# A decode step whose score blocks are turned by VectorE, and whose norm statistics use one small product

## The chip, the cores and the metric

The kernel runs on one core of a Trainium2 chip. The metric is the device time of one execution in microseconds (us). A change of under 0.2% (about 6 us here) can't be told from no change by the measurement that is used.

## The reference

One decoder layer is computed twice: for a prompt of 2048 tokens, and for 8 sequences of 4 new tokens each that look back on 8192 cached tokens. Cut to what matters here:

```python
def rms_norm(x, g):            # mean over the channels of one token
    y = x * lax.rsqrt(jnp.mean(x * x, axis=-1, keepdims=True) + EPS)
    return y * g

def diff_attend(q, k, v, q_pos, k_pos, lam):      # 4 heads, two components c
    s = jnp.einsum('bqhcd,bkhcd->bhcqk', q, k) * (HEAD_DIM ** -0.5)
    s = s - alibi_slopes()[None, :, None, None, None] * dist
    pr = jax.nn.softmax(jnp.where(k_pos <= q_pos, s, -jnp.inf), axis=-1)
    w = pr[:, :, 0] - lam * pr[:, :, 1]
    return jnp.einsum('bhqk,bkhe->bqhe', w, v)

def mixer(xn, lp, ...):
    z = xn @ lp['w_in']                            # q, k, v, and the two halves of a gated unit u
    o = diff_attend(...)                           # past keys and values come from pages
    y_attn = rms_norm(o, lp['g_subln']) * (1.0 - lam_init)          # per head
    c = causal_depthwise_conv(u_ext, lp['w_dw'], lp['b_dw'])        # 31 taps
    y_conv = silu(layer_norm(c, lp['ln_conv_g'], lp['ln_conv_b']))
    return concatenate([y_attn, y_conv]) @ lp['w_out'], ...

def decoder_layer(x, pe, lp, ...):
    h = x + rms_norm(mixer(rms_norm(x, lp['g_pre_mix']), ...), lp['g_post_mix'])
    f = square(relu(rms_norm(h, lp['g_pre_ffn']) @ lp['w_ff1'])) @ lp['w_ff2']
    h = h + rms_norm(f, lp['g_post_ffn'])
    return h + sigmoid(h @ lp['w_ple_gate']) * (pe @ lp['w_ple'])
```

## The kernel before

All activations lie with the channel on the partitions and the token along the free axis, so a norm needs a sum over partitions. Products in full precision are made as three products of two halves each (`mm3`: lines L233, L234, L235), the halves coming from ScalarE (a rounded copy, L120) and VectorE (the rest, L121).

The order of the work is written out by hand. There are three stages. The first (to about 520 us) is the input projection, with `zp` as its PSUM tiles, of which there are four; the convolution, the norm of the four 512-token blocks (`square`, `stat`, `spread`) and the decode tokens' projection run beside it as generators that are advanced a step at a time. The second (to about 1048 us) is the prompt's attention: 64 rows of score tiles (L1214 on TensorE, L1219 on VectorE), turned by TensorE (`tp`, L1278) and multiplied with the values (`ov`, L233 to L235). Its work is a list of pieces; after each piece `advance` gives credit to the decode generator and moves the oldest `subln` by one step. The third is the dense part in five groups of 416 tokens (`mm` tiles): output projection, two MLP products, embedding and gate, with the norms `norm_a` and `norm_f` and the convolution's norm `convln` as side generators.

The decode attention is a generator (`decode`) that runs in the second and third stage. For each of the 8 sequences it visits 16 units of 4 pages: first the keys (`ds`, L992), then after the softmax the values (`dacc`, L1064). Scores of 32 rows (head, component, query) are made in four column tiles of TensorE, one per page of a unit. `weights(u)` turns two units' 128x128 score blocks on TensorE (`dwt`, L1046), and ScalarE copies them out (L1048). In the third stage a key visit takes two units at once (`wide_k`), a value visit one. Each visit returns a cost that is taken from the credit.

`Rstd` makes the inverse root of a mean over partitions. `mean` makes four products with a 128x128 block of the squares as the stationary operand and a column of ones as the moving one (L148, `pm`), which leaves one token per partition; `seed` computes the inverse root with an integer guess and three Newton steps on VectorE or GpSimd (L164 to L181); `spread` turns the four columns, broadcast to 128, back with four transposes on TensorE (L188, `rsb`). It is used 40 times at full width: four blocks in stage one, five times in `convln`, 16 times in `subln` (the norm per head and 512 tokens in stage two), and 15 times in `norm_a` and `norm_f`; and twice for the 32 decode tokens.

`subln` is a generator whose steps are counted by `SL = (8, 2, 10, 0, 1, 1, 0)`: square (L1094), 8 steps, mean, 2 steps, seed, 10 steps, spread and scaling (L1110), two steps, rounding and rest, one step, and then two stores of the tile `o` from GpSimd's queue (L1125). `o` has two buffers; ScalarE fills one in two halves from the single `ov` PSUM tile (L1300).

Of the kernel before, what the change touches and what calls it, by code (L numbers as in the profile page):

```python
# [8 lines left out]
F32 = mybir.dt.float32  # L9
# [40 lines left out]
KC = 1000.0, 2000.0  # L50
C1, C2, C3 = 600.0, 200.0, 1000.0
# [3 lines left out]
C_ID, C_G, C_SEL, C_MC, C_C0, C_C1, C_TX = 0, 128, 256, 288, 304, 305, 306  # L55
NCST = 310
# [77 lines left out]
class Rstd:  # L134
# [5 lines left out]
    def __init__(self, nc, pool, bank, ident, n):  # L140
        self.nc, self.pool, self.bank, self.ident = nc, pool, bank, ident
        self.n, self.w = n, min(128, n)
        self.offs = [min(o, n - self.w) for o in range(0, n, self.w)]

    def mean(self, acc, ones):
        self.pm = self.bank("pm")
        for b, o in enumerate(self.offs):
            self.nc.tensor.matmul(self.pm[:self.w, b:b + 1], acc[:, o:o + self.w], ones, start=True, stop=True)  # L148

    def square(self, eng, inv):  # L150
        self.t = self.pool.tile([128, 4], F32, tag="rst", name="rst", bufs=2)[:self.w, :len(self.offs)]
        eng.tensor_tensor(out=self.t, in0=inv, in1=inv, op=ALU.mult)

    def seed(self, eng, inv=None):

        V, w, nb = self.nc.vector, self.w, len(self.offs)

        def small(tag, bufs=2):
            return self.pool.tile([128, 4], F32, tag=tag, name=tag, bufs=bufs)[:w, :nb]

        x, y = small("rsx"), small("rsy", 4)
        t = self.t if inv is not None else small("rst")
        if inv is None:
            V.tensor_scalar(out=x, in0=self.pm[:w, :nb], scalar1=EPS, scalar2=None, op0=ALU.add)  # L164
        else:
            V.scalar_tensor_tensor(out=x, in0=self.pm[:w, :nb], scalar=2.0 ** 22, in1=t, op0=ALU.mult, op1=ALU.mult)
            V.tensor_scalar(out=x, in0=x, scalar1=EPS, scalar2=None, op0=ALU.add)
# [12 lines left out]
        if inv is not None:  # L180
            eng.tensor_tensor(out=y, in0=y, in1=inv, op=ALU.mult)  # L181
# [11 lines left out]
def kernel(  # L193
# [19 lines left out]
    ones_d = cp.tile([128, 1], F32, name="ones_d")  # L213
    ones_c = cp.tile([128, 128], F32, name="ones_c")
    ones_e = cp.tile([128, 1], F32, name="ones_e")
# [8 lines left out]
    ident = cc[:, C_ID:C_ID + 128]  # L224

# [22 lines left out]
    def convln(pool, bank, n0, n, tags, gated=False):  # L248
# [55 lines left out]
        r = Rstd(nc, pool, bank, ident, n)  # L304
        r.mean(acc, ones_c[:, 0:1])
        r.seed(V)
        yield
        yield
        rsb = r.spread()
        rs = cfull[:, 4, :n]  # L310
        S.activation(out=rs, in_=rsb, func=AF.Copy)
        yield
# [69 lines left out]
    with tc.manual_schedule():  # L382
        nc.sync.dma_start(out=vc, in_=vec)
        V.memset(ones_d, 1.0 / 1024)
        V.memset(ones_c, 1.0 / 512)
        S.activation(out=ones_e, in_=ones_d, func=AF.Copy, scale=8.0)
# [5 lines left out]
        with (  # L392
# [68 lines left out]
            def stat(bl):  # L461
                r = rsd_[bl] = Rstd(nc, p1, st_bank, ident, 512)
                r.mean(sums.pop(bl), ones_d)
                r.seed(V)

            def spread(bl):
                t = rs[bl] = p1.tile([128, 512], F32, tag="rs", name="rs", bufs=2)
                S.activation(out=t, in_=rsd_[bl].spread(), func=AF.Copy)
# [16 lines left out]
            def opening():  # L485
# [10 lines left out]
                spread(0)  # L496
                second(4, 6)
                yield
                second(6, 8)
# [4 lines left out]
                yield  # L504
                spread(1)

            def sumsq(bl):
# [5 lines left out]
                stat(bl)  # L513

# [53 lines left out]
            rd = Rstd(nc, p1, dt_bank, ident, NDEC)  # L568
# [9 lines left out]
            def dec_first():  # L578
                V.tensor_copy(rsb_d, rd.spread())
# [1306 lines left out]
```

## Time and profile before

| | us |
|---|---|
| median of 3 runs | 3206.87 (3205.02 to 3211.97) |
| the profiled execution | 3210.34 |
| its span, first to last instruction | 3208.6 |
| TensorE busy | 3084.4 (96%) |
| VectorE busy | 2027.4 (63%) |
| ScalarE busy | 1258.7 (39%) |
| GpSimd busy | 980.5 (31%) |

The profiled execution is 1.7 us longer than its span and 3.5 us above the median. Matmuls are pipelined: one row's duration is its latency, and the distance between two starts is what it takes from the stream.

### The profile page before, as it was taken

The page shows a single profiled execution, that of the slowest core. Times are in us where ns is not written, and L with a number is a line of the kernel's source. Part 1 is how long each engine was busy: PE and PEld are TensorE (multiplying, and loading weights), DVE is VectorE, ACT ScalarE, POOL GpSimd, SP SyncE. Part 2 cuts the span into 40 slices and gives each one's busy share as a digit, 9 for nine tenths or more (in the row PEclk, how much of TensorE's full clock was granted, in tenths as well). Part 3 has the DMA queues.
Part 4 walks back from the last instruction along what each step waited for, and adds up shares of the span by engine and source line. Part 5 has one row for each costly group of instructions (what it writes and reads, how often), then busy time and mean ns, then how long its engine had stood idle before and what let it go on. Part 6 is the DMA issues. An engine that isn't in the chain of part 4 may idle for free.

```text
span 3208.6 us, 55368 instructions
## 1 busy us (share of the span) xinstructions
PE 3084.4 (96%) x19120; PEld 2694.1 (84%) x19120; DVE 2027.4 (63%) x3537; ACT 1258.7 (39%) x2312; POOL 980.5 (31%) x1063
## 2 busy tenths in 40 slices
PE   8999898999999899989999989999989999999998
PEld 6877686867778688879888879889879999999998
DVE  7889664887784667546767536777538444564444
ACT  5333224776675322235322234322334333432233
POOL 2542213776664301123201124210125121320023
PEclk9999898999899999999999999999999999999999
DMA  5444367998887876776876777777654344333334
GB/s 178 135 125 109 110 183 220 293 282 263 251 273 256 291 237 222 250 258 226 288 238 223 237 258 267 243 235 257 210 185 151 123 140 157 125 117 113 118 117 133
DMA packets 316521, 649.45 MB, mean 202 GB/s; under 512 B 45872, under 2 KB 98864, under 8 KB 315984
## 3 DMA queue, kind: packets, MB, share of 16 engines
q1 hardware_dynamic: 313680, 637.53, 61.9%
q0 software_dynamic: 2560, 8.39, 0.7%
q8 instruction: 150, 2.46, 0.3%
q14 instruction: 131, 1.07, 0.1%
HBM read 581.60 MB, written 64.18 MB: 201 GB/s over the span
## 4 chain that ended last, share of the span: by engine, by line
PE 81%; DVE 8%; DMA 4%; issue 3%; ACT 2%; POOL 2%; SPq 1%; POOLq 0%; DVEq 0%; ACTq 0%
PE mm L233 18%; PE mm L235 18%; PE mm L234 18%; PE zp L233 4%; PE zp L234 4%; PE zp L235 4%; PE dacc L1064 3%; PE ds L992 3%; PE scp L1214 3%; PE tp L1278 1%; DVE wlo L121 1%; PE ov L233 1%; PE pm L148 1%; PE ov L235 1%; PE ov L234 1%
## 5 line engine op out<-in xcount | busy, mean ns | idle before, releaser
L121 DVE TENSOR_TENSOR wlo<-wide 128x1024 fp32r<-128x1024 f32 x410 | 528.6, 1290 | 693.7 <-ACT wide L120 304.5
L233 PE MATMUL mm<-bh,wide 128*128 128x416 f32 x1616 | 584.9, 362 | 22.7 <-ACT wide L120 22.7
L234 PE MATMUL mm<-bh,wlo 128*128 128x416 f32 x1616 | 573.9, 355 | 8.7 <-DVE wlo L121 8.5
L235 PE MATMUL mm<-bl,wide 128*128 128x416 f32 x1616 | 573.9, 355 | 0.0
L120 ACT ACTIVATE wide<-wide 128x1024 fp32r<-128x1024 f32 x410 | 430.6, 1052 | 343.5 <-DMA wide<-ff 220.5
L357 POOL TENSOR_TENSOR r<-r 128x416 f32<-128x416 f32 x160 | 156.1, 977 | 1076.2 <-ACT bh L1572 1076.2
L233 PE MATMUL mm<-xh,wide 128*128 128x416 f32 x1280 | 457.2, 357 | 0.0
L235 PE MATMUL mm<-xl,wide 128*128 128x416 f32 x1280 | 450.6, 352 | 2.5 <-DVE xl L1525 2.5
L234 PE MATMUL mm<-xh,wlo 128*128 128x416 f32 x1280 | 447.9, 350 | 1.0 <-DVE wlo L121 1.0
L233 PEld LDWEIGHTS mm<-bh,wide 128*128 128x128 f32 x1616 | 307.4, 190 | 70.8 <-ACT wide L120 28.3
L234 PEld LDWEIGHTS mm<-bh,wlo 128*128 128x128 f32 x1616 | 307.9, 191 | 18.5 <-DVE wlo L121 13.8
L235 PEld LDWEIGHTS mm<-bl,wide 128*128 128x128 f32 x1616 | 307.1, 190 | 4.6
L233 PEld LDWEIGHTS mm<-xh,wide 128*128 128x128 f32 x1280 | 240.1, 188 | 45.7 <-issue 19.3
L245 DVE SCALAR_TENSOR_TENSOR ct<-ct,vc 128x416 f32<-128x416 f32 x360 | 271.1, 753 | 8.4
L233 PE MATMUL zp<-xh,wh 128*128 128x512 f32 x640 | 260.8, 407 | 8.9 <-ACT wh L120 7.7
L234 PE MATMUL zp<-xh,wl 128*128 128x512 f32 x640 | 254.9, 398 | 8.1 <-DVE wl L121 8.1
L1572 ACT ACTIVATE bh<-r 128x416 fp32r<-128x416 f32 x160 | 88.2, 552 | 434.7 <-DVE r L1571 434.7
L235 PE MATMUL zp<-xl,wh 128*128 128x512 f32 x640 | 255.1, 399 | 3.7 <-DVE xl L529 3.7
L235 PEld LDWEIGHTS mm<-xl,wide 128*128 128x128 f32 x1280 | 240.0, 188 | 6.1 <-DVE xl L1525 3.7
L234 PEld LDWEIGHTS mm<-xh,wlo 128*128 128x128 f32 x1280 | 240.7, 188 | 4.6 <-DVE wlo L121 1.6
L1236 ACT ACTIVATE S<-S,m 128x512 f32<-128x512 f32 (+3 forms) x320 | 206.9, 649 | 43.1 <-DVE m L1219 42.3
L245 DVE SCALAR_TENSOR_TENSOR cv<-u,vc,cv 128x416 f32<-128x416 f32 (+1 forms) x240 | 202.9, 845 | 6.9
(251 smaller groups left out, 5184.7 us busy)
## 6 DMA issues: line engine op xcount, KB each, us to landing
wide<-ff SPq DMA_DIRECT2D x320, 512.0 KB, 4.3
kv<-ck SPq DMA_DIRECT2D x512, 256.0 KB, 3.9
kv<-cv SPq DMA_DIRECT2D x512, 256.0 KB, 3.8
wr<-w_in SPq DMA_DIRECT2D x40, 512.0 KB, 5.7
wide<-w_out SPq DMA_DIRECT2D x40, 512.0 KB, 4.7
wide<-gate SPq DMA_DIRECT2D x40, 512.0 KB, 3.3
wide<-qs SPq DMA_DIRECT2D x64, 256.0 KB, 6.4
ya<-ct SPq DMA_DIRECT2D x40, 208.0 KB, 1.9
```

The costliest lines, as they stand in the source:

```text
L120: self.nc.scalar.activation(out=hi, in_=r, func=AF.Copy)
L121: self.lo_eng(self.ns).tensor_tensor(out=lo, in0=r, in1=hi.bitcast(F32), op=ALU.subtract)
L233: T.matmul(out, wh, xh, start=start, stop=False)
L234: T.matmul(out, wl, xh, start=False, stop=False)
L235: T.matmul(out, wh, xl, start=False, stop=stop)
L245: V.scalar_tensor_tensor(out=c, in0=x, scalar=w, in1=c, op0=ALU.mult, op1=ALU.add)
L357: P.tensor_tensor(out=out, in0=a, in1=b, op=ALU.mult)
L992: T.matmul(ps[32 * s:32 * s + 32, o:o + 128 * n], qz[:, b % 2, h, :], ring[:, g:g + 4 * n - 3:4, h * 128:h * 128 + 128], start=(h == 0), s ...
L1064: T.matmul(acc[32 * s:32 * s + 32, :], wts[u // 2 * 2][:, u % 2, 32 * s:32 * s + 32], t[:, s, :], start=(u == 0), stop=(s > 0 and u == UNI ...
L1214: T.matmul(ps[:, :wp], q[:, c, l, r % 2 * 128:r % 2 * 128 + 128], kt[:, n0 % 1024:n0 % 1024 + wp], start=(l == 0), stop=(l == 1),)
L1236: S.activation(out=st_[c][:, o:e], in_=st_[c][:, o:e], func=AF.Exp, scale=-1.0, bias=st_["m"][:, c, last:last + 1], accum_out=st_["lp"][:, ...
L1572: S.activation(out=ah, in_=r, func=AF.Square)
```

## The change

Decode: the four column tiles of a key product no longer take one page each; tile k takes columns 32k to 32k+31 of all four pages. The score block that results can be turned in blocks of 32x32, so `weights` is one VectorE instruction over two units (128x256) in place of two TensorE transposes and a ScalarE copy. A host table (`tabD`) is permuted to match. Value visits take two units when `wide_k` is set, at a cost of 2000 instead of 2 x 1100.

Norms: `Rstd.gather` turns the squares in 32x32 blocks on VectorE and adds up 32 at a time; `mean` is one product of the constant 0/1 matrix `same` with the 16 (13, 4, 1) partial sums; `spread` is one VectorE turn of a broadcast source. The copies of `rsb` out of PSUM by ScalarE go. The callers put steps between `gather` and `mean`: `subln` gets five more steps, `sumsq` three, the opening one; `rstd` and `convln` keep their number. In `subln` the reciprocal of the row sum, which enters the norm, is now laid out by a VectorE product (`inverse`) and goes through the same TensorE product; its square is a VectorE product too, where GpSimd made it before.

```diff
+VC = 1100.0, 2000.0
-    def mean(self, acc, ones):
+    def gather(self, acc, turned, w=16):
+        V, nb = self.nc.vector, self.nb
+        self.part = self.pool.tile([128, w], F32, tag="rsp", name="rsp", bufs=1)
+        V.transpose(turned, acc)
+        V.tensor_reduce(
+            out=self.part[:, :nb], in_=turned.rearrange("p (b f) -> p b f", f=32), axis=AX.X, op=ALU.add
+        )
+        self.w = nb
+    def inverse(self, eng, inv, own):
+        part = self.part[:, self.nb:2 * self.nb].rearrange("p (r g) -> p r g", g=4)
+        eng.tensor_tensor(
+            out=part, in0=inv.rearrange("p (r o) -> p r o", o=1).to_broadcast([128, 4, 4]),
...
+    def mean(self):
         self.pm = self.bank("pm")
-        for b, o in enumerate(self.offs):
-            self.nc.tensor.matmul(self.pm[:self.w, b:b + 1], acc[:, o:o + self.w], ones, start=True, stop=True)
-    def square(self, eng, inv):
...
+        self.nc.tensor.matmul(self.pm[:, :self.w], self.same, self.part[:, :self.w], start=True, stop=True)
...
+            i = small("rsi", 1)
+            V.tensor_copy(i, self.pm[:, nb:2 * nb])
+            V.tensor_tensor(out=t, in0=i, in1=i, op=ALU.mult)
...
-    def spread(self):
-        r = self.bank("rsb")
-        w = self.w
-        for b, o in enumerate(self.offs):
-            self.nc.tensor.transpose(r[:, o:o + w], self.y[:, b:b + 1].to_broadcast([w, 128]), self.ident[:w, :w])
-        return r[:, :self.n]
+    def spread(self, out):
+        nb = self.nb
+        self.nc.vector.transpose(
+            out.rearrange("p (b f) -> p b f", f=32),
+            self.y.rearrange("p (b o) -> p b o", o=1).to_broadcast([128, nb, 32]),
+        )
+        return out
 # opening(): one step later
                 stat(0)
                 second(2, 4)
                 yield
-                spread(0)
                 second(4, 6)
                 yield
+                root(0)
+                spread(0)
                 second(6, 8)
 # decode(), keys
                     for h in range(NH):
-                        for s in range(4):
-                            g = u % RING * 4 + s
+                        for k in range(4):
                             T.matmul(
-                                ps[32 * s:32 * s + 32, o:o + 128 * n], qz[:, b % 2, h, :],
-                                ring[:, g:g + 4 * n - 3:4, h * 128:h * 128 + 128], start=(h == 0), stop=(h == NH - 1),
+                                ps[32 * k:32 * k + 32, o:o + 128 * n], qz[:, b % 2, h, :],
+                                ring[:, g:g + 4 * n, h * 128 + 32 * k:h * 128 + 32 * k + 32],
+                                start=(h == 0), stop=(h == NH - 1),
                             )
 # decode(), weights
-                    pt_ = spare[0]("dwt")[:, :256].rearrange("p (g q) -> p g q", g=2)
-                    for g in range(2):
-                        o = u * 128 + g * 128
-                        T.transpose(pt_[:, g, :], sc[:, o:o + 128], ident)
                     wt = dc.tile([128, 2, 128], F32, tag="wt", name="wt", bufs=2)
-                    S.activation(out=wt, in_=pt_, func=AF.Copy)
+                    V.transpose(wt[:, :, :].rearrange("p u q -> p (u q)"), sc[:, u * 128:u * 128 + 256])
 # decode(), values
-                for u in range(UNITS):
-                    t = take()
+                u = 0
+                while u < UNITS:
+                    n = 2 if u % 2 == 0 and wide_k else 1
+                    t = [take() for _ in range(n)]
...
-                    yield 1100.0
+                    yield VC[n - 1]
 # subln()
-            r = Rstd(nc, pool, bank, ident, n)
+            r = Rstd(nc, pool, bank, same, n)
+            for _ in range(3):
+                yield 300.0
+            r.gather(sq, b32(yh), 32)
+            for _ in range(2):
+                yield 300.0
             if inv is not None:
-                r.square(eng, inv)
+                r.inverse(V, inv, cc[:, C_OWN:C_OWN + 4])
             for _ in range(SL[0]):
                 yield 300.0
-            r.mean(sq, ones_e)
+            r.mean()
...
-            rs = r.spread()
+            rs = r.spread(bank("rsb")[:, :n])
 # stage three
-            def rstd(st_, wait=1):
-                r = Rstd(nc, p3, st_bank, ident, TG)
-                r.mean(st_["acc"], ones_d)
-                r.seed(V)
-                for _ in range(wait):
-                    yield
-                st_["rs"] = r.spread()
+            def rstd(st_, out=None):
+                r = Rstd(nc, p3, st_bank, same, TG)
+                r.gather(st_["acc"], small("sq", 2))
+                yield
+                r.mean()
+                r.seed(V, 1.0 / 1024)
+                st_["rs"] = r.spread(st_bank("rsb")[:, :TG] if out is None else out[:, :])
```

## Rows read from the trace of the kernel before

**Rows 1.** The page's first part: busy time of each engine, its share of the span, and the number of instructions (PE is TensorE, PEld its weight loads, DVE is VectorE, ACT ScalarE, POOL GpSimd).
```profile
PE 3084.4 (96%) x19120; PEld 2694.1 (84%) x19120; DVE 2027.4 (63%) x3537; ACT 1258.7 (39%) x2312; POOL 980.5 (31%) x1063
```

**Rows 2.** Busy time by stretch: stage one, stage two, the start of stage three, the part of stage three with decode work, the rest, and one start of a head in stage two. Columns: stretch, its length, busy us (and instructions) of PE, PEld, DVE, ACT, POOL, granted TensorE clock, DMA share, GB/s.
```profile
0.00:520.00 520.00, 488.93 (x2405) 391.95 (x2406) 382.82 (x603) 179.83 (x303) 163.47 (x132) 0.97 0.50 143
520.00:1048.00 528.00, 491.06 (x4467) 392.03 (x4469) 384.12 (x1108) 350.44 (x926) 340.85 (x487) 0.97 0.87 269
1048.00:1090.00 42.00, 33.46 (x182) 21.72 (x182) 24.99 (x51) 15.91 (x29) 15.68 (x15) 0.92 0.89 293
1090.00:2400.00 1310.00, 1276.08 (x7868) 1108.16 (x7868) 818.80 (x1209) 420.45 (x637) 265.71 (x257) 0.99 0.72 241
2400.00:3208.00 808.00, 794.89 (x4207) 780.23 (x4206) 416.66 (x567) 292.03 (x417) 194.82 (x174) 1.00 0.40 130
...
900.00:950.00 50.00, 46.73 (x433) 35.61 (x431) 43.10 (x131) 37.56 (x103) 39.75 (x55) 1.00 0.87 273
```

**Rows 3.** Groups of TensorE instructions by line and shape: count, busy us, mean ns of one, idle time before them and what ended it.
```profile
L992 PE MATMUL ds<-kv,qz 128*32 128x256 f32 x1280 | 77.4, 382 | 0.0
L992 PE MATMUL ds<-kv,qz 128*32 128x128 f32 x1536 | 54.6, 278 | 1.4 <-DMA kv<-ck 1.3
L188 PE MATMUL rsb<-cc,rsy 128*128 128x128 f32 x161 | 25.5, 283 | 3.3 <-DVE rsy L175 2.5 <-POOL rsy L181 0.8
L1046 PE MATMUL dwt<-cc,sc 128*128 128x128 f32 x128 | 25.2, 279 | 6.0 <-ACT wt L1048 3.1 <-DVE wtl L1282 2.9
```

**Rows 4.** The instructions on the tile `dacc` by stretch (stage two, then the part of stage three with decode work); columns as in rows 2, with PE, PEld and ACT only. Eight PE rows are one unit of values.
```profile
520.00:1048.00 528.00, 40.31 (x288) 5.88 (x292) 1.16 (x2) 0.97 0.87 269
1048.00:2450.00 1402.00, 109.01 (x756) 16.07 (x756) 3.57 (x6) 0.98 0.72 239
```

**Rows 5.** TensorE in order of time at five places of stage three (equal neighbours are merged): start us, us, engine, line, operation, tiles, shape, count.
```profile
1103.60 0.35 PE L235 MATMUL mm<-xl,wide 128*128 128x416 f32 x1
1103.89 1.06 PE L1064 MATMUL dacc<-kv,wt 128*32 128x512 f32 x8
1104.88 0.46 PE L233 MATMUL mm<-xh,wide 128*128 128x416 f32 x1
...
1254.69 0.36 PE L235 MATMUL mm<-bl,wide 128*128 128x416 f32 x1
1254.88 0.38 PE L1046 MATMUL dwt<-cc,sc 128*128 128x128 f32 x2
...
1256.19 0.45 PE L233 MATMUL mm<-xh,wide 128*128 128x416 f32 x1
...
1457.33 0.60 PE L188 MATMUL rsb<-cc,rsy 128*128 128x128 f32 x4
1457.68 0.43 PE L233 MATMUL mm<-yh,wide 128*128 128x416 f32 x1
...
1623.18 1.04 PE L1070 MATMUL dacc<-vn,wx 4*32 4x512 f32 x2
1624.15 0.38 PE L1072 MATMUL pl<-ls,cc 128*128 128x1 f32 x2
1624.39 0.44 PE L233 MATMUL mm<-bh,wide 128*128 128x416 f32 x1
...
1923.89 0.95 PE L148 MATMUL pm<-ones_d,acc 128*128 128x1 f32 x8
1924.70 0.44 PE L233 MATMUL mm<-yh,wide 128*128 128x416 f32 x1
```

**Rows 6.** Groups of VectorE instructions by line and shape; columns as in rows 3.
```profile
L1253 DVE SCALAR_TENSOR_TENSOR cf<-l,nlam,cf 128x1 f32<-128x1 f32 x64 | 28.5, 445 | 2.2
L1608 DVE TENSOR_TENSOR big<-big,mm 128x416 f32<-128x416 f32 x120 | 69.4, 578 | 3.0 <-PE mm L235 3.0
L167 DVE TENSOR_SCALAR rsx<-rsx 128x4 f32<-128x4 f32 x16 | 9.7, 604 | 0.6
L459 DVE TENSOR_TENSOR shared<-shared 128x512 f32<-128x512 f32 x14 | 9.6, 685 | 0.5
...
L561 DVE TENSOR_REDUCE accd<-xnd 128x32 f32<-128x256 f32 x1 | 0.6, 632 | 0.0
L562 DVE TENSOR_TENSOR xnd<-xd,vc 128x256 f32<-128x256 f32 x1 | 0.4, 427 | 0.0
```

**Rows 7.** VectorE in order of time around 865 us; columns as in rows 5.
```profile
864.82 4.16 DVE L1253 SCALAR_TENSOR_TENSOR cf<-l,nlam,cf 128x1 f32<-128x1 f32 x1
```

**Rows 8.** TensorE in order of time around 870 us; the brackets give the idle time before and what ended it.
```profile
869.99 0.69 PE L1046 MATMUL dwt<-cc,sc 128*128 128x128 f32 x2 [2.86 <-DVE wtl L1282]
```

**Rows 9.** Busy time in the stretch that follows; columns as in rows 2.
```profile
868.80:875.60 6.80, 5.61 (x24) 3.62 (x25) 2.40 (x9) 2.00 (x6) 3.90 (x18) 0.50 0.62 221
```

**Rows 10.** ScalarE in order of time at the first change of heads (the square of the tile `o`, then the copy that fills its buffer next), and such a copy at the third; columns as in rows 8.
```profile
661.37 0.63 ACT L1094 ACTIVATE sq<-o 128x512 f32<-128x512 f32 x1
...
689.64 0.38 ACT L1300 ACTIVATE o<-ov 128x256 f32<-128x256 f32 x1 [3.06 <-DMA ya<-o]
...
931.02 0.38 ACT L1300 ACTIVATE o<-ov 128x256 f32<-128x256 f32 x1 [3.73 <-DMA ya<-o]
```

**Rows 11.** GpSimd at the same change of heads: the store of the tile `o`.
```profile
684.01 0.54 POOL L1125 DMA_DIRECT2D ya<-o  x1
```

**Rows 12.** TensorE at the same change of heads.
```profile
690.08 0.39 PE L233 MATMUL ov<-wth,V 128*128 128x256 f32 x1 [1.41 <-ACT o L1300]
```

More of the change, by code (lines that the diff above doesn't have):

```diff
@@ L154, in seed, with __init__ @@
-    def seed(self, eng, inv=None):
-        V, w, nb = self.nc.vector, self.w, len(self.offs)
-        def small(tag, bufs=2):
[L159 to L164, printed above, removed]
-        else:
-            V.scalar_tensor_tensor(out=x, in0=self.pm[:w, :nb], scalar=2.0 ** 22, in1=t, op0=ALU.mult, op1=ALU.mult)
+    def __init__(self, nc, pool, bank, same, n):
+        self.nc, self.pool, self.bank, self.same = nc, pool, bank, same
+        self.n, self.nb = n, n // 32
@@ new lines, in mean, with seed @@
+    def mean(self):
+        self.pm = self.bank("pm")
+        self.nc.tensor.matmul(self.pm[:, :self.w], self.same, self.part[:, :self.w], start=True, stop=True)
+    def seed(self, eng, scale, inv=False):
+        V, nb = self.nc.vector, self.nb
+        def small(tag, bufs=2):
+            return self.pool.tile([128, 16], F32, tag=tag, name=tag, bufs=bufs)[:, :nb]
+        x, y, t = small("rsx", 1), small("rsy"), small("rst", 1)
+        if not inv:
+            V.tensor_scalar(out=x, in0=self.pm[:, :nb], scalar1=scale, scalar2=EPS, op0=ALU.mult, op1=ALU.add)
+        else:
+            i = small("rsi", 1)
+            V.tensor_copy(i, self.pm[:, nb:2 * nb])
+            V.tensor_tensor(out=t, in0=i, in1=i, op=ALU.mult)
+            V.scalar_tensor_tensor(out=x, in0=self.pm[:, :nb], scalar=scale * 2.0 ** 22, in1=t, op0=ALU.mult, op1=ALU.mult)
@@ L224 @@
     ident = cc[:, C_ID:C_ID + 128]
+    same = cc[:, C_G:C_G + 128]
     def b32(ap):
@@ L303, in convln @@
         yield
-        r = Rstd(nc, pool, bank, ident, n)
-        r.mean(acc, ones_c[:, 0:1])
-        r.seed(V)
+        r = Rstd(nc, pool, bank, same, n)
+        r.gather(acc, tl("sq"))
+        yield
+        r.mean()
+        r.seed(V, 1.0 / 512)
         yield
         yield
-        rsb = r.spread()
-        rs = cfull[:, 4, :n]
-        S.activation(out=rs, in_=rsb, func=AF.Copy)
-        yield
+        rs = r.spread(cfull[:, 4, :n])
         for k in range(5):
@@ L461, in stat, with root @@
             def stat(bl):
-                r = rsd_[bl] = Rstd(nc, p1, st_bank, ident, 512)
-                r.mean(sums.pop(bl), ones_d)
-                r.seed(V)
+                r = rsd_[bl] = Rstd(nc, p1, st_bank, same, 512)
+                r.gather(sums.pop(bl), p1_sq())
+            def root(bl):
+                rsd_[bl].mean()
+                rsd_[bl].seed(V, 1.0 / 1024)
             def spread(bl):
                 t = rs[bl] = p1.tile([128, 512], F32, tag="rs", name="rs", bufs=2)
-                S.activation(out=t, in_=rsd_[bl].spread(), func=AF.Copy)
+                rsd_[bl].spread(t[:, :])
             slow = []
@@ L1062, in decode @@
                         S.activation(out=wx, in_=p4, func=AF.Copy)
[L1063 to L1069 removed]
+                    for i in range(n):
+                        for s in range(4):
+                            T.matmul(
+                                acc[32 * s:32 * s + 32, :], wts[u // 2 * 2][:, u % 2, 32 * s:32 * s + 32], t[i][:, s, :],
+                                start=(u == 0), stop=(s > 0 and u == UNITS - 1),
+                            )
+                        u += 1
+                    for _ in range(n):
+                        stage()
+                    yield VC[n - 1]
                 T.matmul(acc[0:32, :], wx[:, 0:32], vn, start=False, stop=True)
@@ L1532, in norm_a @@
                     yield
-                yield from rstd(nxt)
-                st_["rs2"] = small("rs")
-                S.activation(out=st_["rs2"], in_=nxt["rs"][:, :TG], func=AF.Copy)
+                rs2 = small("rs")
+                yield from rstd(nxt, rs2)
+                st_["rs2"] = rs2
                 yield
```

58 lines of the change are left out of this document (26 added, 32 removed).

## The prediction

> **What bounds the kernel now.** I read the page's first part, then the stretches, then TensorE's groups and its order of time, and last the waits of the engines that the change loads. TensorE is busy 96% of the span, VectorE 63% [rows 1]. By stage TensorE has 489 of 520, 491 of 528, 1276 of 1310 and 795 of 808 us; VectorE has 74%, 73%, 63% and 52% [rows 2]. So in stage three an instruction that leaves TensorE's stream is worth its whole distance to the next one, wherever something else takes its place at once. Stage two is less clear: at a head's start VectorE is at 43.1 of 50 us beside TensorE's 46.7 [rows 2], and there a delay of VectorE may reach TensorE. Because rows of TensorE overlap, I price by the distance between starts, not by the duration.
>
> **What TensorE loses.** Between dense products a full mean takes 1924.70 - 1923.89 = 0.81 us and the four transposes of a spread 1457.68 - 1457.33 = 0.35 us [rows 5]. The one product that replaces the mean has a twin in the kernel: `pl`, the same 0/1 matrix against one column, 1624.39 - 1624.15 = 0.24 us [rows 5]. The new one has up to 32 columns; a bound from below is two of the mean's eight rows, 0.20, and from above the transposes' 0.35, which has 4 x 128 columns. I take 0.24. A statistics set gives back 0.81 - 0.24 + 0.35 = 0.92 us, and there are 40 (the 161 transposes of rows 3 are 40 x 4 and one of the decode tokens): **36.8 us**, of which 4.6 in stage one, 14.7 in stage two, 17.5 in stage three.
>
> A visit to one unit of values takes 1104.88 - 1103.60 = 1.28 us with the dense step before it, and 1256.19 - 1254.69 = 1.50 with the two transposes [rows 5], so these cost 0.22. There are 64 pairs of them [rows 3]: **14.1 us**.
>
> Two units in one visit save the second entry and exit. One unit alone costs 1.28 - 0.19 = 1.09 beyond the stream, where 0.19 is the distance of two starts in the stream (1254.88 - 1254.69); a two-pass product inside a group takes 1624.15 - 1623.18 = 0.97 [rows 5]. So 0.12 per pair. Stage two has 36 units ((292 - 4) / 8, the four being the last product of two sequences) [rows 4], of 128; 92 are left, 46 pairs: **5.5 us**. The lower cost (2000 for 2200) lets decode end sooner, which moves TensorE work but removes none.
>
> The sum of TensorE's side is 56.4 us. In stage two a pair of transposes also waited 2.86 us for a PSUM bank that VectorE held [rows 8], and the granted clock was at its lower level, 0.50, for the 6.8 us behind it [rows 9], which costs 3.4 us. The new turn needs no bank. But VectorE was late because a 128x1 operation took 4.16 us [rows 7], and other work of TensorE needs the same banks, so I count half: **3.1 us**.
>
> **What VectorE gets.** No turn by VectorE and no reduce of 512 columns stand in the trace. The nearest rows: 0.58 us for 416 columns and 0.69 for 512 with two inputs, 0.43 for 256, and a strided reduce of 256 at 0.63, which would be 1.26 for 512 [rows 6]. I take 0.69 for each operation on 512 columns (between 0.58 and 1.26), the row of the same size on the same engine; the strided row is further off, as all three run over columns in order or nearly so. A set then costs 3 x 0.69 = 2.07 us, at 416 columns 1.73; a turn of two units' weights 0.43. In `subln` two small products with two inputs in SBUF come on top. Operations on 4 and 1 columns take 0.60 and 0.45 in this stage [rows 6], once 4.16 [rows 7], so 0.60 each. Stage two gets 16 x (2.07 + 1.2) = 52 us and 19 weight turns, 8 us: 60 in all, between 53 and 92. VectorE idles 528 - 384 = 144 us there [rows 2], so most of it lies in idle time; the cover is three score banks. At a head's start 6.9 us of 50 are idle [rows 2] and about two sets fall there, 6.5 us: the cover is just gone. I charge **8 us**; with the cover gone in half of the stage it would be 30. In stage three VectorE has 491 idle us and gets 33 + 19; I charge nothing there except at the start, below.
>
> The Trainium skill, VectorE: DVE Perf Modes, section Rules for kernel authors, speaks against this part: it gives the turn of a 128x128 block to TensorE where PSUM will do and expects one element a cycle of a reduce. Its section The three transpose paths has 311 ns for a 128x128 bf16 block, an estimate of 1.24 us for 512 columns, and with it stage two would get some 83 us; no run here shows such a turn. By that rule the second rival below would come true.
>
> **What comes later.** ScalarE loses 64 copies and a wait on TensorE, and is not the bound anywhere. In the opening and at the start of stage three TensorE does wait for statistics; there a set's chain becomes 3 x 0.69 - 0.92 = 1.15 us longer (0.81 at 416 columns). Two sets each: 2.3 + 1.6 = **3.9 us**. The opening's later spread leaves the fourth `zp` tile to be filled meanwhile; I charge nothing more.
>
> The step that costs most is the five added ones in `subln`. At the change from the first to the second head the square starts at 661.37 [rows 10] and the store of `o` is issued at 684.01 [rows 11]: 22.6 us for 23 steps, 0.98 each. The tile's next user, ScalarE's copy out of `ov`, waits 3.06 us for that store, 3.73 at the third change [rows 10]; behind it wait the exponentials on ScalarE, and the value products on TensorE, 1.41 us [rows 12]. There is one `ov` tile, so nothing covers it. Five steps more issue the store 4.9 us later, at each of three changes of heads: **14.7 us** of TensorE idle. A wait of 2.86 us was followed by the lower clock [rows 8, 9] and these would be 6; for the two changes that wait already I add 3.4 each, **6.8 us**. In the middle of a head the next user comes many pieces later, and nothing is charged.
>
> **The sum.** 56.4 + 3.1 - 8 - 3.9 - 14.7 - 6.8 = 26.1 us. From the profiled execution's 3210.3 that gives 3184.2; the median of the runs is 3.5 lower, so **3181 us**.
>
> **Rivals.**
> First, all of TensorE's time comes through: the store wait is hidden or short because pieces run faster, and VectorE's load stays in its idle time. Then 56.4 + 6.3 = 62.7 us are the most, 3144; the band is 3144 to 3168. For it: TensorE's 97 to 98% in stage three [rows 2]. Against it: the store wait already stands in the trace [rows 10].
>
> Second, VectorE takes TensorE's place in stage two: half of its 60 us reaches TensorE (30 instead of 8), 3203; at 92 us, 46 instead of 8, 3219. For it: 43.1 of 50 at a head's start; against it: 73% over the stage [rows 2]. It decides once VectorE is late by more than three banks of scores.
>
> Third, and on the other side, slower: the key products read 32 columns at a stretch where they read 128, with four column tiles at once. No row shows such a read. They take 77.4 + 54.6 = 132 us [rows 3]; 20% more undoes the gain, 25% makes it slower by 0.2%, and twice the time would be some 3313. Against it: two stretches far apart (256 columns) take 104 ns longer than one of 128 [rows 3], so a jump costs nothing visible. The Trainium skill, Advanced Engine Details and Errata, section Memory Cachelines, asks only for repeated hits in a 16-byte line, which a run of 32 fp32 values has; by that this rival falls.
>
> Fourth, the change moves TensorE's time without saving it: in stage three waits on weights or VectorE fill what is freed there (17.5 + 9.9 + 5.5 = 32.9 us), which gives 3207 to 3214. Against it: TensorE is hardly ever idle there, and the DMA share is 0.72 [rows 2].
>
> **How the numbers follow.** The forecast, 3168 to 3194, gets 0.45; the first rival 0.25; the second 0.18, of which a third faster by over 0.2%, 0.4 within it, and the rest slower; the third 0.05; the fourth 0.07. Within 0.2% (6.4 us) of 3206.9 is what a measurement can't tell from no change. Faster: 0.45 + 0.25 + 0.06 = 0.76; same 0.07 + 0.05 = 0.12; slower 0.05 + 0.05 + 0.02 = 0.12. The range leaves out the lowest tail of the first rival and what lies past the second's middle: 3146 to 3205. The likeliest case alone has 3168 to 3194.
>
> **What would show it.** Right: no `dwt` and `rsb` rows on TensorE, two rows for each `pm`, value visits of 16 rows, key rows with the old means; VectorE turns near 0.69 us; stage two about as long as before (14.7 + 4.2 + 3.1 saved, 29.5 lost), stage three some 31 us shorter; TensorE's waits for `o` of about 6 us at three changes of heads, with the lower clock behind them. Wrong: turns above 1 us, key rows above their old 382 and 278 ns, a stage two longer by 20 us, or stores that come as early as before.

## The result and the profile after

The changed kernel is slower: 3233.66 us (3231.72 to 3235.47) against 3206.93 for the kernel before on the same chip, a ratio of 1.0077 with a 95% interval of 1.0065 to 1.0089. 3181 us was predicted, 3146 to 3205 the range; the time lies outside it, on the other side.

The page's first part after, where [rows 1] has before:
```profile
PE 3042.9 (94%) x18590; PEld 2658.1 (82%) x18590; DVE 2131.9 (66%) x3773; ACT 1235.1 (38%) x2233; POOL 989.6 (31%) x1047
```
TensorE's busy time fell by 41.5 us and the span grew. What left its stream came back as waiting, and more with it. Where, is seen from the first and last starts of the score products, of the output products (`mm<-yh`) and of the feed-forward products (`mm<-xh`), here before and then after (columns: ns shortest, middle, longest; us of the first and last start):
```profile
L1214 PE MATMUL scp<-wide x224: 274/397/775, 523.7 to 852.4; 128*128 128x512 f32 x88, 128*128 128x256 f32 x16, 128*128 128x384 f32 x8
L1214 PE MATMUL scp<-K,wide x416: 274/393/774, 557.7 to 976.3; 128*128 128x512 f32 x93, 128*128 128x256 f32 x29, 128*128 128x384 f32 x17
L233 PE MATMUL mm<-yh,wide x256: 344/352/462, 1005.3 to 2424.5; 128*128 128x416 f32 x128
L233 PE MATMUL mm<-xh,wide x1280: 344/352/460, 1067.6 to 3069.3; 128*128 128x416 f32 x183
```
```profile
L1247 PE MATMUL scp<-wide x224: 277/397/796, 531.6 to 884.3; 128*128 128x512 f32 x88, 128*128 128x256 f32 x16, 128*128 128x384 f32 x8
L1247 PE MATMUL scp<-K,wide x416: 274/394/796, 566.4 to 1012.6; 128*128 128x512 f32 x93, 128*128 128x256 f32 x29, 128*128 128x384 f32 x17
L251 PE MATMUL mm<-yh,wide x256: 345/352/462, 1044.9 to 2443.0; 128*128 128x416 f32 x128
L251 PE MATMUL mm<-xh,wide x1280: 345/352/548, 1131.7 to 3090.1; 128*128 128x416 f32 x183
```
Stage one ends 7.9 us later (523.7, 531.6). From the first score product to the first output product takes 513.3 us where it took 481.6: 31.7 lost. From there to the first feed-forward product 86.8 instead of 62.3: 24.5 lost. That is 64.1 us; 43.3 of them come back later, so that the last feed-forward product starts 20.8 us late. Two windows after, where [rows 2] has stage two and the start of stage three:
```profile
520.00:1045.00 525.00, 455.59 (x4081) 348.35 (x4080) 415.06 (x1197) 329.93 (x876) 331.54 (x449) 0.94 0.84 251
...
1086.00:1132.00 46.00, 32.63 (x106) 6.73 (x106) 13.06 (x31) 5.27 (x10) 4.28 (x5) 0.93 0.92 296
```
In stage two TensorE now idles 69 us of 525, where it idled 37 of 528; in the second stretch it works 33 of 46.

The groups of the new operations, VectorE and TensorE (the last two answer to `ds` in [rows 3]):
```profile
L150 DVE STREAM_TRANSPOSE yh<-sq 128x512 f32<-128x512 f32 x16 | 11.3, 706 | 17.9 <-DMA ya<-yh 13.5 <-POOL S L371 4.3
L151 DVE TENSOR_REDUCE rsp<-yh 128x16 f32<-128x512 f32 x16 | 11.0, 686 | 0.6
L204 DVE STREAM_TRANSPOSE rsb<-rsy 128x512 f32<-128x512 f32 x16 | 11.4, 714 | 0.0
L1071 DVE STREAM_TRANSPOSE wt<-sc 128x256 f32<-128x256 f32 x64 | 27.9, 436 | 16.9 <-PE dacc L1090 16.9
L159 DVE TENSOR_TENSOR rsp<-inv,cc 128x16 f32<-128x16 f32 x16 | 14.3, 895 | 0.0
L182 DVE TENSOR_TENSOR rst<-rsi 128x16 f32<-128x16 f32 x16 | 10.4, 650 | 0.5
...
L167 PE MATMUL pm<-rsp,cc 128*128 128x13 f32 x40 | 6.1, 227 | 0.0
...
L1017 PE MATMUL ds<-kv,qz 128*32 128x256 f32 x1280 | 77.4, 382 | 0.0
L1017 PE MATMUL ds<-kv,qz 128*32 128x128 f32 x1536 | 54.7, 286 | 4.7 <-DMA kv<-ck 3.1 <-DMA V<-vs 1.6
```
Every operation costs about what was summed. The first row holds the first cause all the same: the turn of `subln` waits 17.9 us, though its input is there.

**Stage two.** VectorE around 836 us, and TensorE's next score products:
```profile
835.92 0.71 DVE L150 STREAM_TRANSPOSE yh<-sq 128x512 f32<-128x512 f32 x1 [4.32 <-POOL S L371]
836.67 0.69 DVE L151 TENSOR_REDUCE rsp<-yh 128x16 f32<-128x512 f32 x1
837.27 0.74 DVE L1252 CUSTOM_DVE_ANT_0 S<-scp,shared,m 128x512 f32<-128x512 f32 x1
```
```profile
838.08 1.22 PE L1247 MATMUL scp<-wide 128*128 128x512 f32 x2 [3.50 <-DVE m L1252]
```
`gather` turns its squares into the tile `yh` (L1127), which has one buffer, and the store of the instance before still reads it. The scores' pass (L1252) stands behind the turn in VectorE's order, and TensorE waits for the scores' pass. A wait of 4.32 us on VectorE becomes one of 3.50 on TensorE. In all TensorE waits 47.2 us there, 18.7 before (us in total, times, longest; before, then after):
```profile
PE scp L1214 <- DVE m L1219: 18.7, 13, 11.2
```
```profile
PE scp L1247 <- DVE m L1252: 47.2, 33, 9.5
```

**The start of stage three.** TensorE in order of time (some rows):
```profile
1085.75 0.35 PE L253 MATMUL mm<-yl,wide 128*128 128x416 f32 x1
1086.03 1.92 PE L1090 MATMUL dacc<-kv,wt 128*32 128x512 f32 x16
...
1119.43 3.93 PE L1090 MATMUL dacc<-kv,wt 128*32 128x512 f32 x8 [4.78 <-DMA kv<-cv]
1123.29 0.60 PE L167 MATMUL pm<-rsp,cc 128*128 128x13 f32 x2
...
1131.68 0.44 PE L251 MATMUL mm<-xh,wide 128*128 128x416 f32 x1
```
For 46 us no dense product runs, only decode visits, some of which wait for their values, and the mean's product. VectorE had turned and reduced the norm's sums by 1106.0, but the mean's product starts at 1123.29, behind the visits. It looks as if data were late. The order is: the last `subln` is appended with a rate of 3 to the list that is stepped once per output block. It needed 24 steps, which eight blocks at 3 give exactly; now it needs 29. The five left over are taken one by one in `first_f1`, and every turn of its loop lets decode advance by 1500.

**Stage one.** Two waits of TensorE on VectorE grew (before, then after):
```profile
268.77 0.38 PE L596 MATMUL dzt<-cc,dzs 128*128 128x32 f32 x2 [1.33 <-DVE qdec L602]
...
337.51 0.79 PE L234 MATMUL zp<-xh,wl 128*128 128x512 f32 x1 [7.66 <-DVE wl L121]
```
```profile
270.69 0.61 PE L620 MATMUL dzt<-cc,dzs 128*128 128x32 f32 x2 [7.03 <-DVE qdec L626]
...
345.66 0.80 PE L252 MATMUL zp<-xh,wl 128*128 128x512 f32 x1 [13.15 <-DVE wl L122]
```

### The profile page after: what moved, and what is told of

It is laid out like the page before. It is cut to its first block, busy times and chain, and to the rows that moved or that the text cites. A ratio compares the mean times of both kernels' runs of the same rounds, so it can differ in the third digit from the quotient of the medians.

```text
span 3229.9 us, 54228 instructions
## 1 busy us (share of the span) xinstructions
PE 3042.9 (94%) x18590; PEld 2658.1 (82%) x18590; DVE 2131.9 (66%) x3773; ACT 1235.1 (38%) x2233; POOL 989.6 (31%) x1047
## 4 chain that ended last, share of the span: by engine, by line
PE 74%; DVE 11%; DMA 5%; POOL 3%; issue 3%; ACT 2%; SPq 1%; POOLq 0%; DVEq 0%; ACTq 0%
PE mm L251 18%; PE mm L252 18%; PE mm L253 18%; PE dacc L1090 3%; PE zp L251 3%; PE ds L1017 3%; PE zp L252 3%; PE zp L253 3%; DVE S L1252 2%; PE scp L1247 2%; DVE wlo L122 1%; DVE cv L263 1%; PE tp L1311 1%; DMA ya<-yh 1%; DVE acd L676 1%
## 5 line engine op out<-in xcount | busy, mean ns | idle before, releaser
L251 PEld LDWEIGHTS mm<-xh,wide 128*128 128x128 f32 x1280 | 243.2, 190 | 21.5 <-issue 15.0
```

Source lines behind the costliest of these rows:

```text
L251: T.matmul(out, wh, xh, start=start, stop=False)
```

## The experiments

Every ratio is to the kernel before on the same chip, with its 95% interval. Where two runs are compared, their median times are subtracted; by the intervals such a difference is uncertain by some 4 to 7 us. Lengths of stages come from the one profiled execution of each run.

### One repair at a time

```
-            side.append([subs.pop(), 3.0, 0.0])
+            side.append([subs.pop(), 4.0, 0.0])
```


> One edit of the changed kernel: the last attention normalisation, which walks beside the output product, is stepped four times per output block instead of three (29 steps are now needed, 24 were before; eight blocks at three give 24). Theory A (the five steps that are left over hold the next stage back, and decode visits that wait for their loads fill the place): the 24.5 us lost between the first output product and the first feed-forward product go down to about 0 to 5; since decode visits done in that place are saved later, the net gain is 8 to 22 us, 3212 to 3226 us. Rival B (the stage starts late because decode or VectorE is behind anyway): that stretch stays within 5 us of what it is, 3230 to 3236 us.

3213.36 us, 1.0014 (1.0005 to 1.0023): 20 us gained. From the first output product to the first feed-forward product it takes 63.7 us, 62.3 before:
```profile
L251 PE MATMUL mm<-yh,wide x256: 345/352/462, 1046.3 to 2424.3; 128*128 128x416 f32 x128
L251 PE MATMUL mm<-xh,wide x1280: 345/352/552, 1110.0 to 3071.1; 128*128 128x416 f32 x183
```
Theory A holds; one number restores the stretch.

```
-            r.gather(sq, b32(yh), 32)
+            r.gather(sq, bank("gt")[:, :n], 32)
```


> One edit of the changed kernel: the attention normalisation turns its squares into a PSUM bank instead of the tile that the store of the instance before it still reads. Theory A (VectorE stands in that wait, 13.5 us and 4.3 us in the profile, and score products queue behind it): the waits of the turn fall below 2 us, TensorE's wait for the scores' VectorE pass falls from 47 us to 25 or less, the attention stage gets 12 to 25 us shorter, 3208 to 3222 us. Rival B (VectorE is simply too full in this stage, so that the wait only moves): the attention stage loses under 6 us, 3227 to 3236 us.

3216.43 us, 1.0035 (1.0021 to 1.0049): 17 us gained. The turn has no wait left, and the wait for the scores' pass is 30.0 us, not quite the 25 expected:
```profile
L150 DVE STREAM_TRANSPOSE gt<-sq 128x512 f32<-128x512 f32 x16 | 11.5, 719 | 0.0
...
PE scp L1247 <- DVE m L1252: 30.0, 32, 10.7
```
Theory A holds. The 4.3 us that the profile puts on GpSimd went too, so they hung on that tile as well.

Both edits together:

> The changed kernel with both edits together: own place for the turned squares, and four steps instead of three at the start of the feed-forward stage. Theory A (two separate causes): the gains of the two runs before, 20 and 17 us, add up, 3192 to 3202 us. Rival B (both edits remove the same stall): 3207 to 3216 us.

3196.45 us, 0.9965 (0.9951 to 0.9979): the gains add up, the causes are separate.

### One half of the change at a time

The kernel before with all lines of the change in `decode` and the table `tabD`; then the changed kernel with these as before.

> The kernel before with the decode part of the change alone (weights turned by VectorE, key reads in the new order, value visits in pairs); the statistics are as before. Theory A (the decode part does what was summed, 14.1 us for the transposes and 46 pairs by 0.23 us, 10.6 us): 3180 to 3190 us. Rival B (the turns on VectorE cost the attention stage what they save on TensorE): 3200 to 3212 us. Rival C (this is the part that makes the change slower): above 3212 us.

> The changed kernel with the decode part as before: only the norm statistics are changed. Theory A (all of the loss is here, since the decode part by itself saves about 20 us): 3245 to 3260 us. Rival B (the statistics save the 37 us that were summed and the decode part loses them): 3165 to 3200 us. Rival C (the two parts only lose together, on VectorE): 3200 to 3225 us.

Decode alone takes 3175.97 us, 0.9902 (0.9887 to 0.9918); the statistics alone 3260.49, 1.0159 (1.0145 to 1.0173). Decode saves 31 us, 4 more than theory A allowed, and the statistics cost 51: theory A in both, each time just past the end of its range. Split again:
```
-                        T.transpose(pt_[:, g, :], sc[:, o:o + 128], ident)
...
+                    V.transpose(wt[:, :, :].rearrange("p u q -> p (u q)"), sc[:, u * 128:u * 128 + 256])
```


> The kernel before with the decode weights turned by VectorE (and the key reads in the order that this needs) alone; values one unit a visit, statistics as before. Theory A (the sum of the prediction, 14.1 us for the transposes and 3.1 for the bank): 3187 to 3192 us. Rival B (the weights give more than was summed, because a pair of transposes also waits for PSUM banks and for ScalarE's copy): 3178 to 3187 us. Rival C (it gives nothing, and the pairs do all): 3200 us and more.

```
-                for u in range(UNITS):
-                    t = take()
+                    n = 2 if u % 2 == 0 and wide_k else 1
+                    t = [take() for _ in range(n)]
```


> The kernel before with the value visits of two units in the feed-forward stage alone; weights turned by TensorE as before. Theory A (0.12 us for each of 46 pairs, as summed): 3199 to 3204 us. Rival B (0.23 us for each, as the order of time of the changed kernel shows): 3194 to 3199 us. Rival C (the lower cost of two units lets decode end earlier, and that gives more): under 3194 us.

The weights give 14 us (3191.45, 0.9955, 0.9941 to 0.9969), the pairs 18 (3186.05, 0.9943, 0.9929 to 0.9956). In the order of time a pair now takes 1084.58 - 1082.42 + 0.19 = 2.35 us with the dense step ahead of it:
```profile
1082.42 0.38 PE L1047 MATMUL dwt<-cc,sc 128*128 128x128 f32 x2
...
1084.58 0.46 PE L234 MATMUL mm<-xh,wide 128*128 128x416 f32 x1
```
Two visits took 1.28 + 1.50, less one step of 0.19: 2.59 [rows 5]. So 0.24 for a pair, 11 us for 46. The time is in rival C's range, but the other 7 us are not accounted for by visits. In the profiled executions five lie ahead of the first output product (1000.4 us against 1005.3), where no pair runs, and may be chance; and from the first feed-forward product to the end TensorE is idle for 43.9 us where it was idle for 49.8. Whether the lower cost of two units brings that wasn't separated.

### Which statistics cost

The attention normalisation as before, all else changed:

> The changed kernel with the attention normalisation (its statistics and its steps) as before; the statistics of the opening, of the convolution norm and of the feed-forward stage stay changed, and so does decode. Theory A (what is lost in the attention stage and at the start of the feed-forward stage belongs to this one place): the attention stage lasts as long as with the decode part alone, the first feed-forward product follows the first output product by 60 to 66 us, the opening keeps its loss of 8 us, and the later statistics save 6 to 18 us: 3166 to 3180 us. Rival B (the turns of the feed-forward stage cost as well): 3184 to 3200 us.

3181.83 us, 0.9919 (0.9907 to 0.9932): 2 us past theory A's end and under rival B's. With this one place undone the kernel is 52 us faster. The first feed-forward product follows the first output product by 63.9 us, as theory A has it, but the attention stage, from the first score product to the first output product, lasts 482.1 us, 7 longer than with decode alone (475.1). The opening undone instead, on top of both repairs:

> The changed kernel with both edits, and the statistics of the opening (both of its blocks of tokens, the later sums and the decode tokens) as before. Theory A (the opening's loss of 8 us comes from VectorE, which is late there by the turns): the last projection product starts 6 to 8 us earlier and the time is 3187 to 3192 us. Rival B (the convolution norm in the opening does it, or the time is given back later): within 3 us of the kernel with both edits, 3193 to 3200 us.

3183.73 us, 0.9931 (0.9918 to 0.9945): 12.7 us, more than the 8 expected; the two waits of stage one are back at 1.26 and 7.66 us. In the profiled executions the score products start 8.7 us earlier (522.2 against 530.9), and the attention stage is 5 us shorter too (495.4 against 500.4): the new statistics of the opening cost something in the stage behind it as well, which also fits most of the 7 us above. And of it the decode tokens' statistic alone:

> The changed kernel with both edits and the decode tokens' statistic in the opening as before; the blocks' statistics there stay changed. Theory A (the decode tokens' part makes VectorE late for the products behind it): 3183 to 3189 us, as with the whole opening undone (3184). Rival B (the blocks' turns do it, which stand in VectorE's order ahead of the weights' low halves): 3193 to 3199 us, as with both edits alone (3196).

3195.41 us, 0.9963 (0.9949 to 0.9976): nothing gained, the waits stay at 5.51 and 13.15. Rival B: the statistics of the blocks of tokens do it. Whether by their turns or by the three steps that `sumsq` got wasn't separated.

Only the feed-forward stage's statistics, beside decode; only the convolution norm's in that stage; and both:

> Decode changed, and of the statistics only those of the feed-forward stage (two for each group of tokens and the last ones); opening, convolution norm and attention normalisation as before. Theory A (TensorE is the bound in this stage and VectorE has room, so each statistic gives its 0.9 us back): 5 to 15 us under the run with decode alone, 3161 to 3171 us. Rival B (the turns sit in the chain that the next group waits for): 3176 to 3190 us.

> The decode part alone, and of the statistics only those of the convolution norm in the feed-forward stage (four of them). Theory A (these four stand where VectorE has room; two runs that differ by the convolution norm and the opening differ by 8 us between the first feed-forward product and the end): 3 to 8 us under the decode part alone, 3168 to 3173 us. Rival B (those 8 us come from the later start alone): 3174 to 3179 us.

> The decode part, and the statistics of the feed-forward stage with its convolution norms; opening and attention normalisation as before. Theory A (between the first feed-forward product and the end the kernel with only these norms and the attention part takes 2100 us, decode alone 2114, so there are some us to be had): 3165 to 3171 us. Rival B (waits on weights and VectorE fill what is freed): 3172 to 3179 us.

3178.36 (0.9911, 0.9899 to 0.9924), 3173.81 (0.9901, 0.9886 to 0.9916) and 3173.28 us (0.9897, 0.9881 to 0.9912), where decode alone has 0.9902: no difference that is larger than the intervals. The first and the last time lie in rival B's ranges, the second between its two theories; a gain of some us can't be ruled out. From the first feed-forward product to the end, in decode alone and then with both:
```profile
1061.70:3175.90 2114.20, 2069.03 (x12097) 1904.55 (x12096) 1252.77 (x1839) 707.11 (x1022) 463.92 (x436) 0.99 0.60 202
```
```profile
1063.20:3168.80 2105.60, 2050.11 (x11917) 1883.27 (x11916) 1288.38 (x1893) 703.86 (x1014) 470.50 (x436) 0.99 0.60 202
```
TensorE's busy time falls by 18.9 us and VectorE's grows by 35.6, but TensorE is idle for 10.3 us more (55.5 against 45.2). The stretch is 8.6 us shorter in these two executions, which lie 7 us apart, where the medians lie 2.7 apart. The waits on the weight stream grow (decode alone, then both):
```profile
PE mm L234 <- ACT wide L121: 22.4, 6, 7.0
PE mm L235 <- DVE wlo L122: 10.0, 16, 1.0
```
```profile
PE mm L311 <- ACT wide L121: 26.4, 9, 7.0
PE mm L312 <- DVE wlo L122: 17.4, 18, 3.2
```
That is 11.4 us, about all of the added idle time: more than half of what left TensorE's stream came back as these waits. 7.4 of them are for the low halves of the weights (`wlo`), which VectorE makes in order; that a turn with its reduce (1.2 us) stands ahead of them is the likely reason and wasn't tested.

### What the repaired attention normalisation still costs

> The decode part, and of the statistics only the attention normalisation, with both repairs (turned into a PSUM bank, four steps at the start of the next stage). Theory A (VectorE's added work in the attention stage is not covered): 3180 to 3188 us, with TensorE's wait for the scores' VectorE pass near 30 us where decode alone has 21. Rival B (once repaired it costs nothing; the rest came together with the opening): 3172 to 3178 us.

3197.12 us, 0.9964 (0.9951 to 0.9978): 20 us over decode alone, more than the 4 to 12 of theory A's range. Then with the work of VectorE doubled at that place:
```
+            gt = bank("gt")[:, :n]
+            for _ in range(2):
+                r.gather(sq, gt, 32)
```


> As e_subln_fixed, with the turn and the reduce issued twice in each attention normalisation: 16 times 0.71 + 0.69 us, 22 us more on VectorE and nothing more on TensorE. Theory A (TensorE is held by VectorE's amount of work there): 6 to 14 us above e_subln_fixed. Rival B (the amount is covered, it is the chain's steps that cost): within 3 us of it.

3207.56 us, 0.9997 (0.9988 to 1.0006): 10.4 us more for 22.4 us of VectorE's work, 0.46 us for each, and by the intervals 0.2 to 0.7. The attention stage itself is 16.4 us longer in the profiled executions (509.6 against 493.2), 0.73 for each. The waits for the scores' pass in decode alone, with the repaired normalisation, and doubled:
```profile
PE scp L1219 <- DVE m L1224: 21.2, 15, 10.7
```
```profile
PE scp L1301 <- DVE m L1306: 31.7, 34, 9.6
```
```profile
PE scp L1303 <- DVE m L1308: 45.5, 41, 9.5
```
Theory A holds: the amount is not covered. Not all of it goes by the scores' pass. TensorE's transposes `tp` wait 6.2 us in the doubled run and 0.3 in the other for the reduce, which holds a PSUM bank of theirs; and with the repaired normalisation the value products wait for VectorE's `wtl`, which in decode alone they don't:
```profile
PE ov L313 <- DVE wtl L1369: 8.7, 5, 3.4
```
The other doubt was whether the small products have to be on VectorE:
```
-                r.inverse(V, inv, cc[:, C_OWN:C_OWN + 4])
+                r.inverse(eng, inv, cc[:, C_OWN:C_OWN + 4])
...
-            V.tensor_tensor(out=t, in0=i, in1=i, op=ALU.mult)
+            eng.tensor_tensor(out=t, in0=i, in1=i, op=ALU.mult)
```


> As the kernel with both edits, and the spread of the reciprocals over 16 columns (0.895 us mean, up to 3.55 us) and their squares (0.650 us, up to 1.72 us) on GpSimd instead of VectorE. Theory A (these two stand on VectorE until GpSimd's instruction in flight ends: short ones take 0.13 to 0.18 us, the long ones all overlap a GpSimd instruction; and VectorE is what the scores wait for): 6 to 15 us under the kernel with both edits. Rival B (they only lengthen the chain in GpSimd's order, or VectorE's time there is covered): within 4 us of it, or above.

3193.34 us, 0.9959 (0.9946 to 0.9972), 3 us under the kernel with both edits, with intervals that overlap: rival B. Their 24.7 us on VectorE in the changed kernel are not worth 0.46 each. The trace shows why: most of that time is a wait for GpSimd's addition in flight (the last section), and with the products gone another VectorE operation with two inputs in SBUF takes it over. GpSimd and VectorE in this run:
```profile
639.10 4.56 POOL L371 TENSOR_TENSOR S<-S,S 128x2048 f32<-128x2048 f32 x1
```
```profile
640.53 3.14 DVE L1286 SCALAR_TENSOR_TENSOR cf<-l,nlam,cf 128x1 f32<-128x1 f32 x1
```
The 64 operations `cf` take 15.4 us with both edits and 24.0 here; before the change they took 28.5 [rows 6]. The value products still wait 7.0 us for `wtl`, where the kernel with both edits has 8.8.

On top of the later stages' new statistics the same repaired normalisation costs 10 us by the medians (3173.28 and 3183.73, the run with the opening undone, which has the new statistic in the opening's convolution norm too), not 20. The traces don't show that difference: the attention stage is 18 us longer in both pairs of profiled executions (493.2 against 475.1, 495.4 against 477.1), and the whole executions are 14 and 12 us longer. The intervals allow one value for both.

No version with the new attention statistics beats the one without them. Decode alone beats both kernels, at 0.990, and nothing that was added to it beats it clearly.

## Why the prediction was wrong

**The bound.** Right for TensorE, and that is why decode pays. The 43.1 of 50 us of VectorE at a head's start [rows 2] was the right warning.

**TensorE's terms.** The operations left as said. The 14.1 us of the transposes and half of the bank's wait: 17.2 forecast, 14 measured. Pairs: 5.5 forecast, 18 measured. The working took 0.97 for a product inside a group as a second visit, where the distance between starts gives 0.24 a pair, 11 us; the rest is open. The 36.8 us of the statistics failed as a term of time: in stage three 18.9 us left the stream, near the 17.5 that were summed, and 11.4 came back as waits on the weight stream. There the fourth rival came true in part, against the argument that TensorE was hardly ever idle. That it has no idle time says that nothing else is late now, not that nothing is late next.

**VectorE's prices.** Right: turns 0.706 to 0.714 us, reduce 0.686, weights 0.436 against 0.69, 0.69 and 0.43. By the rule of the Trainium skill that was weighed (VectorE: DVE Perf Modes, The three transpose paths) 512 columns were an estimate of 1.24 us; the rows say 0.71. The two small products took 0.90 and 0.65 in the mean against 0.60, which looks near. But the mean hid the matter: the 64 operations `cf` of [rows 6] with a mean of 0.45 have a median of 0.22 and a longest of 4.20, and the first product has a median of 0.17 and a longest of 3.55. The 4.16 of [rows 7] was read as one late operation, where it was a wait for GpSimd (the last section) that the new products ran into too.

**VectorE in stage two.** This step failed in two ways. First, 8 of 60 us were charged. The doubled run prices VectorE's work at 0.46 there, or at 0.73 by the stage's own length. An instance gets 0.71 + 0.69 + 0.71 + 0.90 + 0.65 = 3.66 us; 16 of them 59, and at these prices some 27 to 43, against 14.7 saved on TensorE. That is an estimate of 12 to 28 us of loss, where the stage lost 18 and the time 10 to 20; the two small products count for less, since `cf` fell from 28.5 to 15.2 us at the same time. The second rival named this, with 30 for the 8, and had 0.18. Second, the wait on `yh` wasn't seen at all: 17 us. The change allocates the tile ahead of the gather instead of behind the spread, in these lines:
```
+            yh = pool.tile([128, 512], F32R, tag="syh", name="yh")[:, :n]
...
-            rs = r.spread()
-            yh = pool.tile([128, 512], F32R, tag="syh", name="yh")[:, :n]
```
That a tile with one buffer was thereby wanted while its last store was under way could be read there.

**The five steps.** Counted rightly, followed to the wrong place. 14.7 + 6.8 us were charged for the store of `o` at changes of heads. ScalarE's waits for it came to 6.8 us before and to 7.3 after, where the charge adds 14.7. At the first change:
```profile
704.29 0.38 ACT L1333 ACTIVATE o<-ov 128x256 f32<-128x256 f32 x1 [2.70 <-DMA ya<-o]
```
has 2.70 us where [rows 10] has 3.06. TensorE's waits for `o` fell from 5.2 to 1.7 us, and with both repairs, when VectorE holds the score products for less, they are 4.6: the charge of 21.5 us was for something that didn't happen. The square stands at 675.2 and the store at 698.8, 23.6 us for 28 steps, where 22.6 went to 23: the steps are paced by pieces, and the price of 0.98 each was no constant. What came instead was the last instance, which falls out of the eight blocks that carried it: 20 us, which the prediction didn't have.

**The opening.** 2.3 us were charged for the chain; 13 were lost, 8.7 of them in the opening and 5 in the attention stage in the profiled executions, on work behind VectorE and not on the chain.

**The rivals.** None whose cause occurred reaches 3233.7: the second ends at 3219, the fourth at 3214, and neither the shared tile nor the last instance stood in any. Slower had a chance of 0.12. The key reads cost nothing: 382 and 286 ns against 382 and 278 [rows 3]. The way back in runs: decode alone 3176.0; 7.8 for the repaired normalisation with the later statistics, 3183.7; 12.7 for the opening, 3196.5; 37.2 for the two faults, 3233.7.

## What to carry to other kernels

Before moving work from a full engine to a half idle one, ask what on the receiving engine's queue is wanted at once: turns by VectorE paid in decode, and a set of turns, a reduce and small products cost in the attention stage, where it stands ahead of what TensorE waits for. When steps are added to a hand-paced sequence, divide its new length by each place's rate: the instance at the edge of a stage is the one that falls over. And for every scratch tile ask who reads it last: here the turn waited 13.5 us for stores of its tile to land.

## What the runs showed of the hardware

A product of 16 columns on VectorE with both inputs in SBUF took from 0.13 us to 3.55 us. GpSimd and VectorE around 641 us, and the same product at 706 us, in the changed kernel:
```profile
640.66 4.57 POOL L371 TENSOR_TENSOR S<-S,S 128x2048 f32<-128x2048 f32 x1
```
```profile
641.11 0.68 DVE L1315 TENSOR_TENSOR wtl<-tp,wth 128x512 fp32r<-128x512 f32 x1
641.71 3.55 DVE L159 TENSOR_TENSOR rsp<-inv,cc 128x16 f32<-128x16 f32 x1
...
706.39 0.13 DVE L159 TENSOR_TENSOR rsp<-inv,cc 128x16 f32<-128x16 f32 x1
```
The long one ends at 645.26, 0.03 us behind GpSimd's addition (645.23); the two others above 3.5 us do the same. The short one ran while GpSimd was idle. Ahead of the long one, during the same addition, the subtraction `wtl`, with one input in PSUM, kept its 0.68 us. The 4.16 us of [rows 7] end in the same way, at 868.98, 0.02 us behind this addition in the kernel before:
```profile
864.43 4.53 POOL L354 TENSOR_TENSOR S<-S,S 128x2048 f32<-128x2048 f32 x1
```
The Trainium skill, SBUF — State Buffer (section SBUF: two separate sides), says that a VectorE instruction with two SBUF inputs and a GpSimd instruction that reads SBUF share a pair of ports, which the one that starts first holds for its whole length; the rows agree.
